# Output projection as seven products of quarter matrices instead of eight

## The chip, the cores and the metric

The kernel runs on one core of one Trainium2 chip. The metric is the device time of one execution in microseconds (us). The engines are named as in the profile: PE is TensorE's matmul, PEld its weight load, DVE is VectorE, ACT is ScalarE, POOL is GpSimd, and SP is SyncE, which here only issues transfers (DMAs).

## What is computed

One layer of a decoder trunk over 1024 positions of width 1024, all in float32. Two token mixers (A and B) give `y_A` and `y_B`, learned gates merge them, and the merged matrix is projected. The change is in that projection and in what feeds it:

```python
m_a, m_b = jnp.split(jax.nn.sigmoid(h @ w_merge[i]), 2, axis=-1)
out = (m_a * y_a + m_b * y_b) @ w_out[i]          # (1024, 1024) @ (1024, 1024)
x = x + rmsnorm(out, g_post[i])
e = p[i] @ w_ple[i]
gate = jax.nn.sigmoid(x @ w_ple_gate[i])
x = x + rmsnorm(gate * e, g_ple[i])
```

## The kernel before

**How it is scheduled.** The kernel writes its operations into a list (`Program`, lines 198 to 552), and a planner (`schedule`, from line 301) turns the list into a fixed order for each engine. The planner takes the operation that can start first by its own costs and latencies, places tiles in two arenas in on-chip memory (`arena_r` for float32r operands, `arena_f` for float32) and in the eight banks of PSUM (`arena_p`), and keeps to the quotas of the table `QUOTA`. `BASE` gives each part its rank. All instructions are emitted from line 521, so the profile has one line for nearly everything, and a reader goes by engine, tile and shape. An engine runs its own list in order: an instruction that waits holds up all that stand behind it.

**Precision by three products.** A float32 matrix is split in a high part (a cast to float32r) and a low part (source minus high), by `split_w` for a source in on-chip memory and `split_p` for one in PSUM. The cast may go to ACT or DVE, and `split_w`'s subtraction to POOL or DVE, as the planner likes. `mm3` then issues three matmuls. A block of 128 rows by 512 columns with a depth of 1024 thus takes 24 matmuls of 512 columns.

**The parts of the program.** `p2_block` and `score_block` (parts "x" and "s", the first 110 us) make the keys and the sparse-attention scores: for each of eight row blocks a projection of 208 columns, a chain of small DVE operations on it (names `wi`, `fb`, `cs`), transposes, then the score matmuls, which ACT passes through a Relu and DVE adds up. `v_b`, `q_a`, `gates_a`, `merge_gates`, `pair_b`, `top_k` and `mixer_a` fill the middle. Then, for each half `t` of the rows, `y_A` and `y_B` are made in 8 column blocks, merged and split into `mt`. A small product (`pe`) follows, then the output projection: columns in two halves `q`, for each half eight row blocks `b`, each 24 matmuls into one bank, then

```python
        V.scalar_tensor_tensor(x1[b][:, cq], ps, 0.25, gpb[:, cq], op0=ALU.mult, op1=ALU.mult)
        A.activation(jo, ps, AF.Square, scale=0.25, accum_out=s1[:, b, q:q + 1])
```

With the second half a block's norm is finished, the residual `x` is loaded and added, and the result is transposed and split into `xT`, which the last stage (the gate with `w_ple_gate`, 16 blocks of 24 matmuls) reads. `load_q` loads half of a weight matrix in four transfers of 512 KB and splits it.

Of the kernel before, what the change touches and what calls it, by code (L numbers as in the profile page):

```python
# [12 lines left out]
F32 = mybir.dt.float32  # L13
F32R = mybir.dt.float32r
# [536 lines left out]
class _Eng:  # L551
# [11 lines left out]
    "hT": (64, 0, 1, 64, 1), "w2": (14, 0, 0, 14, 1), "wn": (36, 1, 1, 16, 1), "vbt": (8, 1, 0, 4), "W": (16, 0, 0, 4, 1),  # L563
    "Wm": (16, 0, 0, 12), "ki": (8, 0, 0, 8, 1), "hlt": (8, 1, 0, 4, 1), "qs": (6, 1, 0, 4, 1), "kt": (4, 1, 0, 4, 1),
    "B": (48, 1, 0, 32), "pt": (12, 1, 0, 4), "kva": (12, 0, 1, 12), "qsa": (8, 1, 0, 6), "att": (64, 0, 1),
# [9 lines left out]
}  # L575

BASE = {"x": -1, "s": 0.3, "vb": 0.3, "qa": 0.3, "ga": 2.7, "mg": 5.3, "pair": 2, "top": 2.7, "A": 4.7, "end": 6}
STEP = 100000
N_IDLE = 8

# [2 lines left out]
def hybrid_block_kernel(ctx: ExitStack, tc: tile.TileContext, x, p, w_in, b_forget, w_branch_a,  # L583
# [606 lines left out]
    def mixer_a():  # L1190
# [6 lines left out]
        for i in range(NB):  # L1197
# [36 lines left out]
            for g in range(4):  # L1234
                split_w(u4[:, g], at[0, g, 0, t][:, cs_], at[0, g, 1, t][:, cs_])

    pg.at("vb", None)
    v_b()
    pg.at("qa", None)
# [12 lines left out]
    mixer_a()  # L1252


    mt = [[[pg.tile([P, 4, 512], F32R, f"m{t}", f"m{t}{e}{g}") for g in range(2)] for e in range(2)] for t in range(2)]
    for t in range(2):
        pg.at("end", 7 + t)
        c = slice(t * 512, t * 512 + 512)
        for g in range(4):
            for e in range(2):  # L1260
                at[1, g, e, t] = pg.tile([P, 512], F32R, "att", f"at1{g}{e}{t}")
                G.dma_start(at[1, g, e, t], att_d[e][g][t])
        for j in range(8):
            wb = [load_wT(w[0, :, j * P:(j + 1) * P], 4, f"wbr{n}_{j}{t}", "Wb") for n, w in
                  enumerate((w_branch_a, w_branch_b))]
            ths = []
            for mi in range(2):
                th = pg.tile([P, 512], F32, "th", f"thl{mi}_{j}_{t}")
                SY.dma_start(th, th_d[mi][j][:, c])
                ths.append(th)  # L1270
            for mi in (1, 0):
                ps = pg.psum([P, 512], "d", f"y{mi}_{j}_{t}")
                for k in range(4):
                    mm3(ps, *wb[mi][k], at[mi, k, 0, t], at[mi, k, 1, t],
                        k == 0, k == 3, [ths[mi]] if k == 0 else ())
                V.scalar_tensor_tensor(ths[mi], ths[mi], 1.0, ps, op0=ALU.add, op1=ALU.mult)
            V.tensor_add(ths[0], ths[0], ths[1])
            split_w(ths[0], mt[t][0][j // 4][:, j % 4], mt[t][1][j // 4][:, j % 4])


    QW = 512
# [1 line left out]
    def load_q(src, q, name):  # L1283
        ws = []
        sv = src.rearrange("(k p) c -> p k c", p=P)
        for k in range(0, KC, 2):
            w = pg.tile([P, 2, 2, QW], F32R, "wo", f"{name}{k}")
            st = pg.tile([P, 2, QW], F32, "st", f"{name}s{k}")
            SY.dma_start(st, sv[:, k:k + 2, q * QW:(q + 1) * QW], hold=[w])
            split_w(st, w[:, 0], w[:, 1])  # L1290
            ws += [(w[:, 0, 0], w[:, 1, 0]), (w[:, 0, 1], w[:, 1, 1])]
        return ws
# [42 lines left out]
    pg.at("end", 10)
    wq, begun = {}, []
    for q, b in order:
        if q not in wq:
            wq[q] = load_q(w_out[0], q, f"wo{q}")
        cq = slice(q * QW, (q + 1) * QW)  # L1340
        ps = pg.psum([P, 512], "d", f"out{q}_{b}")
        begun.append(len(pg.ops))
        t, bs = b // 4, slice((b % 4) * P, (b % 4 + 1) * P)
        for k in range(KC):
            mm3(ps, mt[t][0][k // 4][:, k % 4, bs], mt[t][1][k // 4][:, k % 4, bs], *wq[q][k],
                k == 0, k == KC - 1, [x1[b]] if k == 0 else ())
        V.scalar_tensor_tensor(x1[b][:, cq], ps, 0.25, gpb[:, cq], op0=ALU.mult, op1=ALU.mult)
        A.activation(jo, ps, AF.Square, scale=0.25, accum_out=s1[:, b, q:q + 1])
        if q == 1:
            xb = []  # L1350
            for g in range(2):
                xb.append(pg.tile([P, 512], F32, "xr", f"xr{b}{g}"))
                SY.dma_start(xb[g], x[0, b * P:(b + 1) * P, g * 512:(g + 1) * 512])
            V.tensor_add(s1[:, b, 4:5], s1[:, b, 0:1], s1[:, b, 1:2])
            A.activation(s1[:, b, 5:6], s1[:, b, 4:5], AF.Sqrt, scale=1.0 / D, bias=eps_t)
            V.reciprocal(s1[:, b, 4:5], s1[:, b, 5:6])
            for g in range(2):
                xg = x1[b][:, g * 512:(g + 1) * 512]
                V.scalar_tensor_tensor(xg, xg, s1[:, b, 4:5], xb[g], op0=ALU.mult, op1=ALU.add)
                pt = pg.psum([P, 4, P], "t", f"xt{b}_{g}")  # L1360
                with pg.group():
                    for c in range(4):
                        T.transpose(pt[:, c], x1[b][:, (4 * g + c) * P:(4 * g + c + 1) * P], ident)
                split_p(pt, xT[t][0][g][:, :, bs], xT[t][1][g][:, :, bs])


    C3 = 0.375 ** 6
# [16 lines left out]
    for n, (q, b) in enumerate(order):  # L1384
        if q not in wq:
            wq[q] = load_q(w_ple_gate[0], q, f"wg{q}")
        cq = slice(q * QW, (q + 1) * QW)
        t, bs = b // 4, slice((b % 4) * P, (b % 4 + 1) * P)
        ps = pg.psum([P, 512], "d", f"pg{q}_{b}")
        begun.append(len(pg.ops))  # L1390
        for k in range(KC):
            mm3(ps, xT[t][0][k // 4][:, k % 4, bs], xT[t][1][k // 4][:, k % 4, bs], *wq[q][k],
                k == 0, k == KC - 1)
        gv = gvs[q, b] = pg.tile([P, QW], F32, "gv", f"gv{q}_{b}")
        SY.dma_start(gv, ge_d[b][:, cq])
        pg.ops[-1].deps.add(begun[13 + n])
        th = pg.tile([P, QW], F32, "gt", f"gt{q}_{b}")
        A.activation(th, ps, AF.Tanh, scale=0.5)
        last = q == 1 and b == NB - 1
        if last:  # L1400
            A.activation(warm, th[:, 0:1], AF.Sqrt, scale=0.0, bias=eps_t)
        V.scalar_tensor_tensor(gv, th, 1.0, gv, op0=ALU.add, op1=ALU.mult)
        if q == 1:
            V.tensor_tensor_reduce(out=jo, in0=gv, in1=gv, scale=0.25, scalar=s2[:, b, 0:1], op0=ALU.mult, op1=ALU.add,
                                   accum_out=s2[:, b, q:q + 1])
        else:
            A.activation(jo, gv, AF.Square, scale=0.5, accum_out=s2[:, b, q:q + 1])
# [59 lines left out]
```

## Time and profile before

| | |
|---|---|
| median of three runs (lowest, highest) | 1111.01 us (1108.54, 1111.92) |
| the profiled execution's own time | 1111.12 us |
| its span in the trace | 1109.4 us |
| PE busy, DVE busy, ACT busy, POOL busy | 97%, 72%, 54%, 12% of the span |
| mean granted clock of TensorE | 0.986 of full speed |

The span runs from the first to the last recorded instruction; 1.7 us of the time lie outside it. Busy shares are means over stages with different limits, so a stage is read by its own window.

### The profile page before, as it was taken

To read this page: it belongs to the slowest core of one execution; us is meant where nothing else is said; L and a number is where in the kernel's file an instruction comes from. 1 tells how busy PE (TensorE), PEld (TensorE's weight loads), DVE (VectorE), ACT (ScalarE), POOL (GpSimd) and SP (SyncE) were. 2 spreads that over 40 slices of the span, in tenths; PEclk is the share of its full clock that TensorE was granted. 3 is DMA by queue.
4 is the path that set the end of the run, shared out by engine and by line. 5 is a ranking of instruction groups with operands and counts; after the bars stand their busy time and mean duration, and the time that the engine had idled before them with its cause. 6 is when DMAs were issued, how large, how long until landed. Compare 5 with 4: busy or idle time off the path is not lost. (4 is left out here: it accounts for less than half of the span.)

```text
span 1109.4 us, 16308 instructions
## 1 busy us (share of the span) xinstructions
PE 1073.3 (97%) x5290; PEld 882.7 (80%) x5290; DVE 802.1 (72%) x2086; ACT 603.8 (54%) x1396; POOL 133.2 (12%) x244
## 2 busy tenths in 40 slices
PE   8899999999999999999999999999999999999995
PEld 6777887887878878788878888888888888887884
DVE  6999667757969878799999957655388732366277
ACT  6565578888889889775278855432112131233212
POOL 1413000010111211211411200000100000000011
PEclk8999999999999999999999999999999999998998
DMA  7212033370361622635243422333786273026032
GB/s 264 70 37 67 11 138 119 134 180 10 102 156 39 159 70 82 150 97 178 95 124 97 122 64 79 106 113 106 227 247 200 77 242 109 29 72 202 31 111 99
DMA packets 117594, 128.00 MB, mean 115 GB/s; under 512 B 11642, under 2 KB 78330, under 8 KB 117508
## 3 DMA queue, kind: packets, MB, share of 16 engines
q1 hardware_dynamic: 105940, 108.60, 30.7%
q0 software_dynamic: 11568, 18.35, 7.1%
q8 instruction: 42, 0.69, 0.3%
q14 instruction: 44, 0.36, 0.1%
HBM read 89.60 MB, written 33.13 MB: 111 GB/s over the span
## 5 line engine op out<-in xcount | busy, mean ns | idle before, releaser
L521 PE MATMUL arena_p<-arena_r 128*128 128x512 f32 (+5 forms) x4384 | 1016.0, 385 | 17.1 <-DVE arena_r L521 6.5
L521 PEld LDWEIGHTS arena_p<-arena_r 128*128 128x128 f32 x4384 | 783.8, 190 | 175.6 <-DVE arena_r L521 11.3
L521 ACT ACTIVATE arena_f<-arena_p 128x512 f32<-128x512 f32 (+5 forms) x188 | 97.9, 533 | 205.9 <-PE arena_p L521 123.7
L521 DVE TENSOR_TENSOR arena_r<-arena_p,arena_r 128x512 fp32r<-128x512 f32 (+3 forms) x232 | 141.7, 622 | 48.4 <-ACT arena_r L521 44.7
L521 ACT CAST arena_r<-arena_p 128x512 fp32r<-128x512 f32 (+4 forms) x217 | 107.3, 516 | 117.7 <-PE arena_p L521 114.1
L521 ACT ACTIVATE arena_f<-arena_f,cnd 128x1024 bf16<-128x1024 f32 (+4 forms) x160 | 149.7, 936 | 31.9 <-DVE cnd L521 28.1
L521 ACT ACTIVATE arena_f<-arena_f,stats 128x512 f32<-128x512 f32 (+3 forms) x192 | 116.9, 611 | 21.2 <-DVE stats L521 15.8
L521 DVE TENSOR_TENSOR arena_r<-arena_f,arena_r 128x512 fp32r<-128x512 f32 (+4 forms) x200 | 120.0, 612 | 4.3 <-ACT arena_r L521 1.0
L521 PE MATMUL arena_p<-ident,arena_f 128*128 128x128 f32 x720 | 110.7, 276 | 1.8 <-DVE arena_r L521 0.6
L521 POOL TENSOR_TENSOR arena_r<-arena_f,arena_r 128x512 fp32r<-128x512 f32 (+2 forms) x51 | 65.4, 1289 | 366.2 <-ACT arena_r L521 111.4
L521 PEld LDWEIGHTS arena_p<-ident,arena_f 128*128 128x128 f32 x720 | 87.4, 142 | 24.0 <-DVE arena_f L521 2.3
L521 ACT CAST arena_r<-arena_f 128x512 fp32r<-128x512 f32 (+3 forms) x104 | 55.1, 561 | 69.2 <-DVE arena_f L521 45.8
L521 DVE CAST arena_r<-arena_f 128x512 fp32r<-128x512 f32 (+3 forms) x147 | 55.1, 384 | 41.5 <-DMA arena_f<-in_w_out_dram 15.2
L521 DVE CUSTOM_DVE_ANT_0 arena_f<-arena_p,arena_f 128x512 f32<-128x512 f32 (+2 forms) x112 | 64.1, 577 | 2.6 <-PE arena_p L521 1.5
L521 DVE SCALAR_TENSOR_TENSOR arena_f<-arena_f,wi 128x384 f32<-128x384 f32 (+3 forms) x70 | 48.3, 696 | 13.4 <-ACT arena_f L521 12.6
L521 POOL TENSOR_SCALAR_AFFINE_SELECT arena_f<-arena_f 128x128 f32<-128x128 f32 x70 | 22.5, 323 | 260.5 <-DVE stats L521 112.8
L521 DVE SCALAR_TENSOR_TENSOR arena_f<-arena_f,arena_p 128x512 f32<-128x512 f32 x48 | 32.8, 683 | 28.9 <-PE arena_p L521 22.1
L521 DVE CAST arena_r<-arena_p 128x512 fp32r<-128x512 f32 (+4 forms) x67 | 40.8, 612 | 17.7 <-PE arena_p L521 17.4
L521 ACT COPY arena_f<-arena_p 64x256 f32<-64x256 f32 (+5 forms) x85 | 37.8, 445 | 21.7 <-PE arena_p L521 17.9
L521 DVE SCALAR_TENSOR_TENSOR arena_f<-arena_f 128x512 f32<-128x512 f32 (+7 forms) x47 | 29.0, 623 | 26.5 <-ACT arena_f L521 25.6
L521 DVE TENSOR_TENSOR arena_f<-arena_f 128x512 f32<-128x512 f32 (+3 forms) x101 | 45.0, 446 | 1.3 <-DMA arena_f<-rd_d 0.5
L521 DVE CUSTOM_DVE_ANT_0 arena_f<-arena_p,arena_f,stats 128x384 f32<-128x384 f32 (+2 forms) x64 | 39.3, 615 | 6.9 <-PE arena_p L521 3.6
(103 smaller groups left out, 486.1 us busy)
## 6 DMA issues: line engine op xcount, KB each, us to landing
arena_f<-in_w_in_dram SPq DMA_DIRECT2D x56, 256.0 KB
arena_f<-in_w_merge_dram SPq DMA_DIRECT2D x32, 256.0 KB
th_d<-arena_f SPq DMA_DIRECT2D x32, 256.0 KB
arena_f<-th_d SPq DMA_DIRECT2D x32, 256.0 KB
arena_f<-in_x_dram SPq DMA_DIRECT2D x18, 256.0 KB
vb_d<-arena_r SPq DMA_DIRECT2D x8, 512.0 KB
qsa_d<-arena_r SPq DMA_DIRECT2D x16, 256.0 KB
arena_f<-negc_d SPq DMA_DIRECT2D x8, 512.0 KB
```

The source lines that it names most:

```text
L521: getattr(eng[x], m)(*[real(q) for q in a], **{n: real(q) for n, q in k.items()})
```

## The change

The projection is cut into quarters: the merged matrix A (1024 rows by 1024) into A11, A12, A21, A22 and `w_out` into B11 to B22, each 512 by 512. A product of two quarters takes 4 row blocks of 12 matmuls of 512 columns. Eight such products with four sums of results become seven products of sums of quarters (Winograd's form), with sums before and after:

- T1 to T4 are sums of weight quarters. `weight_sums` makes them early in the program: for each of four row groups `k` two transfers of 512 KB from `w_out`, four subtractions of 128 by 512 on GpSimd, and one transfer of 1 MB to a buffer `tw_d` in DRAM.
- S1 to S4 are sums of quarters of A, made after the merge for the second half of the rows by `either` (GpSimd or DVE). Seven left operands of four tiles are split instead of four.
- `quad` loads one weight quarter or sum in two transfers of 512 KB and splits it; `product` makes one row block. The results are added with `add_to` (DVE, reads PSUM and on-chip memory) into `x1`.
- The squares for the norm now read `x1`, and the weight `g_post` (`gpb`, scaled once) is multiplied in with the norm in `first_residual`, so the residual is added by a separate operation.

```diff
+    pg.at("tw", None)
+    tw_d = [pg.dram(dr, [P, 4, 4, 512], "tw_d0")]
+    def weight_sums(w, dst):
+        for k in range(4):
+            b4 = pg.tile([P, 4, 512], F32, "tw", f"tw{k}")
+            for g in range(2):
+                SY.dma_start(b4[:, 2 * g:2 * g + 2].rearrange("p a b -> p (a b)"), w[(4 * g + k) * P:(4 * g + k + 1) * P, :])
+            G.tensor_sub(b4[:, 0], b4[:, 1], b4[:, 0])
+            G.tensor_sub(b4[:, 1], b4[:, 3], b4[:, 1])
+            G.tensor_sub(b4[:, 3], b4[:, 3], b4[:, 0])
+            G.tensor_sub(b4[:, 2], b4[:, 2], b4[:, 3])
+            SY.dma_start(dst[:, k], b4)
...
-            V.tensor_add(ths[0], ths[0], ths[1])
-            split_w(ths[0], mt[t][0][j // 4][:, j % 4], mt[t][1][j // 4][:, j % 4])
+            m = mq[t][j]
+            V.tensor_add(m, ths[0], ths[1])
+            if t == 0:
+                left["A11" if j < 4 else "A12"].append(halves(m, "mA", f"mA{j}"))
+            elif j < 4:
+                either("tensor_sub", s3[j], mq[0][j], m)
+            else:
+                q = j - 4
+                either("tensor_add", mq[1][q], mq[1][q], m)
+                either("tensor_sub", mq[0][q], m, s3[q])
+                either("tensor_sub", mq[0][j], mq[0][j], mq[0][q])
...
+    def product(lw, i, ws, name, hold=()):
+        ps = pg.psum([P, 512], "d", f"{name}_{i}")
+        for k in range(4):
+            h_, l_ = lw[k]
+            bs = slice(i * P, (i + 1) * P)
+            mm3(ps, h_[:, bs], l_[:, bs], *ws[k], k == 0, k == 3, hold if k == 0 else ())
+        return ps
...
+    def add_to(out_, ps, part):
+        V.scalar_tensor_tensor(out_, ps, 1.0, part, op0=ALU.mult, op1=ALU.add)
...
+    ws = wquad("B11")
+    for i in range(4):
+        A.copy(part[i], product(left["A11"], i, ws, "P1", [x1[4 + i]]))
+    ws = wquad("B21")
+    for i in range(4):
+        add_to(x1[i][:, q0], product(left["A12"], i, ws, "P2", [x1[i]]), part[i])
+        square(i, 0)
+    ws = wquad("T2")
+    for i in range(4):
+        add_to(part[i], product(left["S2"], i, ws, "P6"), part[i])
+    ws, ws2 = wquad("T1"), wquad("B22")
+    for i in range(4):
+        add_to(late[i], product(left["S1"], i, ws, "P5"), part[i])
+        add_to(x1[i][:, q1], product(left["S4"], i, ws2, "P3"), late[i])
+        square(i, 1)
+        first_residual(i)
+    ws = wquad("T3")
+    for i in range(4):
+        ps = product(left["S3"], i, ws, "P7")
+        add_to(late[i], ps, late[i])
+        add_to(part[i], ps, part[i])
+        square(4 + i, 1)
+    ws = wquad("T4")
+    for i in range(4):
+        add_to(part[i], product(left["A22"], i, ws, "P4"), part[i])
+        square(4 + i, 0)
+        first_residual(4 + i)
```

The tables change with it: the buffer for the residual `x` (`"xr"`) grows from 2 to 4 KB, `"we"` from 12 to 16 KB, `"m0"` and `"m1"` give way to `"mA"`, `"mS"` and `"mq"`, and `"tw"` has 8 KB, one tile of four sums.

**What moves.** The planner makes a new order for every engine, since it is greedy and the early part differs. On GpSimd's list, in the first 110 us, these are the rows from the end of the setup to the selects on the first scores (`AFFINE_SELECT`); a row that writes `arena_r` is the low part of a split, one that writes `arena_f` from `arena_f` is a sum of weight quarters:

```order
 L521 TENSOR_TENSOR arena_r<-arena_f,arena_r 128x4x128
-L521 TENSOR_TENSOR arena_r<-arena_f,arena_r 128x512 x9
-L521 TENSOR_TENSOR arena_r<-arena_f,arena_r 128x4x64 x3
+L521 TENSOR_TENSOR arena_r<-arena_f,arena_r 128x512
+L521 TENSOR_TENSOR arena_f<-arena_f 128x512
+L521 TENSOR_TENSOR arena_r<-arena_f,arena_r 128x512 x2
+L521 TENSOR_TENSOR arena_f<-arena_f 128x512 x3
+L521 TENSOR_TENSOR arena_r<-arena_f,arena_r 128x512 x3
+L521 TENSOR_TENSOR arena_f<-arena_f 128x512 x4
+L521 TENSOR_TENSOR arena_r<-arena_f,arena_r 128x4x64
 L521 AFFINE_SELECT arena_f<-arena_f 128x128
+L521 TENSOR_TENSOR arena_f<-arena_f 128x512 x4
```

The 16 sums stand in four batches of four among the early splits (the last batch follows behind the next select), and some of the splits' low parts have gone to DVE.

On SP's list, at the end of the output projection, these are the rows before of the residual loads (`in_x`) and of the first weights of the gate (`in_w_ple_gate`):

```order
L521 DMA arena_f<-in_x_dram 128x512 x8
L521 DMA arena_f<-ge_d_156 128x512
L521 DMA arena_f<-in_x_dram 128x512 x2
L521 DMA arena_f<-ge_d_157 128x512
L521 DMA arena_f<-in_x_dram 128x512 x2
L521 DMA arena_f<-ge_d_158 128x512
L521 DMA arena_f<-in_x_dram 128x512
L521 DMA arena_f<-in_w_ple_gate_dram 128x2x512 x2
```

And these after:

```order
L521 DMA arena_f<-in_x_dram 128x512 x4
L521 DMA arena_f<-tw_d_146 128x2x512
L521 DMA arena_f<-in_x_dram 128x512 x3
L521 DMA arena_f<-in_w_ple_gate_dram 128x2x512
L521 DMA arena_f<-in_x_dram 128x512
L521 DMA arena_f<-in_w_ple_gate_dram 128x2x512 x3
```

Before, 14 of the 16 residual loads stand ahead of the gate's first weights (one of them further up); after, nine do (two of them further up), and the four transfers of the gate's first half follow almost at once.

## Rows read from the trace of the kernel before

**Rows 1.** The page: busy time of TensorE's matmuls, share, instructions

```profile
PE 1073.3 (97%) x5290; PEld 882.7 (80%) x5290; DVE 802.1 (72%) x2086; ACT 603.8 (54%) x1396; POOL 133.2 (12%) x244
```

**Rows 2.** Waits of PE, whole span: us in total, times, longest

```profile
PE arena_p L521 <- DVE arena_r L521: 10.0, 13, 2.7
PE arena_p L521 <- DVE arena_f L521: 7.3, 8, 2.4
```

**Rows 3.** Windows: length, busy (instructions) by engine, PEclk, DMA share, GB/s

```profile
50.00:100.00 50.00, 49.34 (x251) 38.50 (x250) 46.23 (x172) 30.36 (x77) 10.25 (x11) 1.00 0.21 59
850.00:1015.00 165.00, 161.13 (x728) 130.97 (x727) 83.25 (x135) 40.17 (x88) 2.60 (x2) 0.98 0.35 117
```

**Rows 4.** Timeline of PE: start, length, instructions [idle before <-releaser]

```profile
899.17 61.93 PE L521 MATMUL arena_p<-arena_r 128*128 128x512 f32 x272 [0.23 <-DVE arena_r L521]
...
1004.56 0.80 PE L521 MATMUL arena_p<-arena_r 128*128 128x512 f32 x1 [2.34 <-DVE arena_r L521]
1005.75 2.50 PE L521 MATMUL arena_p<-arena_r 128*128 128x512 f32 x5 [0.40 <-DVE arena_r L521]
...
1015.07 81.21 PE L521 MATMUL arena_p<-arena_r 128*128 128x512 f32 x357
```

**Rows 5.** Windows of 3 us where the granted clock is low

```profile
109.00:112.00 3.00, 2.60 (x11) 2.37 (x12) 2.89 (x6) 1.74 (x4) 1.88 (x1) 0.65 0.00 0
112.00:115.00 3.00, 3.00 (x16) 2.67 (x15) 1.65 (x4) 0.98 (x2) 0.00 (x0) 0.78 0.02 5
...
1006.00:1009.00 3.00, 3.00 (x10) 2.41 (x11) 1.49 (x2) 0.00 (x0) 0.00 (x0) 0.50 0.72 208
1009.00:1012.00 3.00, 3.00 (x11) 2.35 (x11) 2.20 (x3) 0.59 (x1) 0.00 (x0) 0.66 0.88 322
```

**Rows 6.** Timeline of POOL, 30 to 110 us

```profile
31.29 1.29 POOL L521 TENSOR_TENSOR arena_r<-arena_f,arena_r 128x512 fp32r<-128x512 f32 x1 [1.52 <-ACT arena_r L521]
33.27 7.33 POOL L521 TENSOR_TENSOR arena_r<-arena_f,arena_r 128x512 fp32r<-128x512 f32 x5 [0.69 <-ACT arena_r L521]
50.25 1.34 POOL L521 TENSOR_TENSOR arena_r<-arena_f,arena_r 128x512 fp32r<-128x512 f32 x1 [9.66 <-DVE arena_r L521]
56.05 1.29 POOL L521 TENSOR_TENSOR arena_r<-arena_f,arena_r 128x512 fp32r<-128x512 f32 x1 [4.46 <-ACT arena_r L521]
...
103.93 3.25 POOL L521 TENSOR_TENSOR arena_r<-arena_f,arena_r 128x512 fp32r<-128x512 f32 x2 [3.08 <-DVE arena_r L521]
```

**Rows 7.** Timeline of DVE, 30 to 110 us

```profile
31.48 2.48 DVE L521 TENSOR_TENSOR arena_r<-arena_p,arena_r 128x512 fp32r<-128x512 f32 x4
...
35.56 1.23 DVE L521 TENSOR_SCALAR wi<-arena_f 128x8 f32<-128x8 f32 x1
...
40.87 0.15 DVE L521 TENSOR_SCALAR wi<-arena_f 128x8 f32<-128x8 f32 x1
...
103.71 0.61 DVE L521 SCALAR_TENSOR_TENSOR arena_f<-arena_f,wi 128x384 f32<-128x384 f32 x1
...
104.38 1.66 DVE L521 SCALAR_TENSOR_TENSOR arena_f<-arena_f,wi 128x384 f32<-128x384 f32 x1
```

**Rows 8.** Timeline of PE, 40 to 110 us

```profile
42.81 0.73 PE L521 MATMUL arena_p<-identr,arena_r 128*128 128x128 f32 x4 [2.69 <-DVE arena_r L521]
...
59.60 0.28 PE L521 MATMUL arena_p<-identr,arena_r 128*128 128x128 f32 x1 [0.16 <-DVE arena_r L521]
...
109.40 0.62 PE L521 MATMUL arena_p<-arena_r 128*128 128x384 f32 x2 [1.89 <-ACT arena_f L521]
```

**Rows 9.** DVE by form, 840 to 1015 us: busy us, mean ns of one

```profile
L521 DVE TENSOR_TENSOR arena_r<-arena_f,arena_r 128x1024 fp32r<-128x1024 f32 x12 | 14.6, 1220 | 0.3
...
L521 DVE SCALAR_TENSOR_TENSOR arena_f<-arena_p,arena_f 128x512 f32<-128x512 f32 x16 | 11.1, 692 | 36.0 <-PE arena_p L521 34.7 <-ACT arena_f L521 0.9
...
L521 DVE TENSOR_TENSOR arena_f<-arena_f 128x512 f32<-128x512 f32 x9 | 6.2, 688 | 0.2
```

**Rows 10.** Transfers, 0 to 64 us in 40 slices: GB/s

```profile
GB/s 0 252 191 320 133 312 379 412 412 231 323 415 415 399 327 45 0 0 0 0 0 10 10 0 0 41 0 0 103 126 343 206 283 87 37 91 82 51 75 48
```

More of the change, by code (lines that the diff above doesn't have):

```diff
@@ L572 @@
     "x1": (32, 0, 1, 32), "gv": (24, 1, 0, 18), "es": (8, 1, 0, 2), "g": (4, 1, 0), "pb": (2, 1, 0, 1), "gt": (4, 1, 0, 2),
[1 row of a table removed]
[1 row of a table added]
     "o": (12, 1, 0, 2), "d": (8, 0, 0, 2, 1), "is": (2, 1, 0, 2, 1), "pe": (8, 1, 0, 2), "rk": (6, 1, 0, 6),
 }
[L577 removed]
+BASE = {"x": -1, "s": 0.3, "vb": 0.3, "qa": 0.3, "ga": 2.7, "mg": 5.3, "tw": 4.0, "pair": 2, "top": 2.7, "A": 4.7, "end": 6}
 STEP = 100000
@@ L1252, in hybrid_block_kernel, with halves @@
     mixer_a()
-    mt = [[[pg.tile([P, 4, 512], F32R, f"m{t}", f"m{t}{e}{g}") for g in range(2)] for e in range(2)] for t in range(2)]
+    def halves(src, grp, name):
+        hl_ = [pg.tile([P, 512], F32R, grp, f"{name}{e}") for e in range(2)]
+        split_w(src, *hl_)
+        return hl_
+    mq = [[pg.tile([P, 512], F32, "mq", f"mq{t}{j}") for j in range(8)] for t in range(2)]
+    s3 = [pg.tile([P, 512], F32, "mq", f"ms{j}") for j in range(4)]
+    left = {n: [] for n in ("A11", "A12", "S1", "S2", "S3", "S4", "A22")}
     for t in range(2):
@@ L1333, in hybrid_block_kernel @@
     jo = pg.tile([P, QW], BF16, "jk", "jo")
-    order = [(q, b) for q in range(2) for b in range(NB)]
[L1335 to L1364, printed above, removed]
@@ new lines, in hybrid_block_kernel, with quad @@
+    V.tensor_scalar_mul(gpb, gpb, 0.25)
+    pg.at("end", 10)
+    for n, src in (("S2", mq[0][:4]), ("S1", mq[1][:4]), ("S4", mq[0][4:]), ("S3", s3), ("A22", mq[1][4:])):
+        for k in range(4):
+            left[n].append(halves(src[k], "mS", f"{n}{k}"))
+    begun = []
+    def quad(w, tw, n):
+        ws = []
+        for k in range(0, 4, 2):
+            if n[0] == "B":
+                g, q = int(n[1]) - 1, int(n[2]) - 1
+                src = w.rearrange("(k p) c -> p k c", p=P)[:, 4 * g + k:4 * g + k + 2, q * 512:q * 512 + 512]
+            else:
+                src = tw[:, k:k + 2, ("T1", "T3", "T4", "T2").index(n)]
+            wt = pg.tile([P, 2, 2, 512], F32R, "wo", f"w{n}{k}")
+            st = pg.tile([P, 2, 512], F32, "st", f"w{n}s{k}")
+            SY.dma_start(st, src, hold=[wt])
+            split_w(st, wt[:, 0], wt[:, 1])
+            ws += [(wt[:, 0, 0], wt[:, 1, 0]), (wt[:, 0, 1], wt[:, 1, 1])]
+        return ws
@@ new lines, in product, with square, first_residual @@
+    def product(lw, i, ws, name, hold=()):
+        ps = pg.psum([P, 512], "d", f"{name}_{i}")
+        begun.append(len(pg.ops))
+        for k in range(4):
+            h_, l_ = lw[k]
+            bs = slice(i * P, (i + 1) * P)
+            mm3(ps, h_[:, bs], l_[:, bs], *ws[k], k == 0, k == 3, hold if k == 0 else ())
+        return ps
+    def square(b, q):
+        A.activation(jo, x1[b][:, q * 512:q * 512 + 512], AF.Square, scale=0.25, accum_out=s1[:, b, q:q + 1])
+    def first_residual(b):
+        t, bs = b // 4, slice((b % 4) * P, (b % 4 + 1) * P)
+        xb = []
+        for g in range(2):
+            xb.append(pg.tile([P, 512], F32, "xr", f"xr{b}{g}"))
+            SY.dma_start(xb[g], x[0, b * P:(b + 1) * P, g * 512:(g + 1) * 512])
+        V.tensor_add(s1[:, b, 4:5], s1[:, b, 0:1], s1[:, b, 1:2])
+        A.activation(s1[:, b, 5:6], s1[:, b, 4:5], AF.Sqrt, scale=1.0 / D, bias=eps_t)
+        V.reciprocal(s1[:, b, 4:5], s1[:, b, 5:6])
+        for g in range(2):
+            xg = x1[b][:, g * 512:(g + 1) * 512]
+            V.scalar_tensor_tensor(xg, xg, s1[:, b, 4:5], gpb[:, g * 512:(g + 1) * 512], op0=ALU.mult, op1=ALU.mult)
+            either("tensor_add", xg, xg, xb[g])
+            pt = pg.psum([P, 4, P], "t", f"xt{b}_{g}")
+            with pg.group():
+                for c in range(4):
+                    T.transpose(pt[:, c], x1[b][:, (4 * g + c) * P:(4 * g + c + 1) * P], ident)
+            split_p(pt, xT[t][0][g][:, :, bs], xT[t][1][g][:, :, bs])
@@ new lines, in add_to, with wquad @@
+    def add_to(out_, ps, part):
+        V.scalar_tensor_tensor(out_, ps, 1.0, part, op0=ALU.mult, op1=ALU.add)
+    def wquad(n):
+        return quad(w_out[0], tw_d[0], n)
+    q0, q1 = slice(0, 512), slice(512, 1024)
+    part, late = [x1[4 + i][:, q0] for i in range(4)], [x1[4 + i][:, q1] for i in range(4)]
+    ws = wquad("B11")
[5 more added lines that the diff above has]
+        square(i, 0)
@@ L1395, in hybrid_block_kernel @@
         SY.dma_start(gv, ge_d[b][:, cq])
-        pg.ops[-1].deps.add(begun[13 + n])
+        pg.ops[-1].deps.add(begun[25 + n])
         th = pg.tile([P, QW], F32, "gt", f"gt{q}_{b}")
```

1 line of the change is left out of this document (added), and 6 rows, old and new, of the table QUOTA.

## The prediction, made before the change was run

> **What bounds the kernel now.** I read the page first: TensorE's matmuls are busy for 1073.3 of 1109.4 us [rows 1]. The list of what TensorE waited for comes next. Its two largest entries, 17.3 us in 21 waits, both name VectorE [rows 2]. So the end is set by the amount of matmul work and by the places where VectorE is late. The windows then show where VectorE has room: hardly any in 50 to 100 us (46.23 of 50 busy), much from 850 to 1015 us, where the change adds its sums (83.25 of 165) [rows 3].
>
> The reader should see two more things. First, where TensorE stands still for 2 us or so, its granted clock may fall behind the wait. The 1.89 us wait at 109.40 [rows 8] is followed by two windows at 0.65 and 0.78, and the 2.34 and 0.40 us at 1004 [rows 4] by 0.50 and 0.66 [rows 5]; 0.50 is the lower level (1.2 of 2.4 GHz) throughout. The 2.69 us at 42.81 had no such price. Second, GpSimd and VectorE get in each other's way. While GpSimd subtracts 128x512 tiles (five from 33.27 to 40.6 us; one alone takes 1.29) [rows 6], VectorE's little operation on `wi` takes 1.23 us, and the same operation 0.15 us at 40.87, just after GpSimd stopped; an addition of scores takes 1.66 instead of 0.61 us when GpSimd runs its pair at 103.93 [rows 6, 7]. The difference, 1.05 to 1.08 us, is a standstill. VectorE's operations that read PSUM are spared: four from 31.48 to 33.96 took 0.62 us each, with GpSimd at work to 32.58 and from 33.27 [rows 6, 7].
>
> **The change, part by part.**
>
> *Matmuls.* Seven products of 48 take the place of eight, and the order shows 48 matmuls of 512 columns fewer, 3680 for 3728, with every other form unchanged. In the unbroken run of the gate 357 took 81.21 us, 0.2275 each; the projection gives the same (272 in 61.93) [rows 4]. That is **-10.9 us**, all on the path, because TensorE is the busy engine there (161.13 of 165) [rows 3].
>
> *The early sums.* The loads and stores are 8 MB in the first 110 us. The queue is nearly empty from 25 to 44 us, but moves some 400 GB/s before that [rows 10]; the first 1 MB comes behind the last `x` and would cost 2.6 us at that rate if it delayed work. I take 0, since the pieces of `w_in` behind it are wanted only by the score products at 48 us. The first store, 1 MB, waits on SP for its batch of sums; behind it stand a `w_in` piece and the key stores, wanted later still. Also 0.
>
> The price is VectorE's. Sixteen subtractions of 1.29 us stall it by at most 16 x 1.08 = 17.3 us. Four low parts fewer go to GpSimd in this stretch and cost VectorE 0.61 each instead of a 1.08 stall: 1.9 back, so 15.4 net, and at the lower end 0, where VectorE would have been idle. How much TensorE pays, batch by batch:
>
> - Batch 1. The run of splits that ended at 40.6 gets four sums and loses one split; one sum fits in a gap. Two more stalls, 2.2 us, and TensorE was already waiting there (2.69 at 42.81 [rows 8]), so all of it counts.
> - Batch 2 falls in the chain of small operations on `p2_block`, 43 to 60 us. It stalls 4.3 us; the splits at 50.25 and 56.05 move away (-2.2) and two of them cost VectorE 0.61 each (+1.2). Of the 3.3 us, TensorE has 1.4 of cover: the new order puts 57 instead of 51 matmuls of 512 columns between the transposes of this stretch. The two single stalls before cost TensorE only 0.16 us (59.60 [rows 8]), so a little slack exists. I take 2.0.
> - Batches 3 and 4 fall among the score additions. The nearest row is the pair at 103.93, which was followed by TensorE's 1.89 us wait for ScalarE, itself held up by VectorE [rows 6, 8]. Four in a row cost at least that, at most 4.3. I take 1.9 each, the lower end, because VectorE was not quite full there, and 1.0 back because the pair itself moves.
>
> Together **+7.0 us**, bounds 0 and 15.4. For the clock behind such waits I add one fall like that at 109: (0.35 + 0.22) x 3 us = **+1.7** [rows 5], bounds 0 and 3.4.
>
> *Sums, splits and squares at the end.* VectorE gets 12 more additions from PSUM (0.692), 27 more of 128x512 (0.688), five more low parts of that size and three of 1024 columns (1.220): 8.3 + 18.6 + 3.4 + 3.7, some 34 us [rows 9]; five casts fewer are left out. From 850 to 1015 it is busy 83.25 [rows 3], so some 117 of the 154 that are left there: hidden on the whole. In the alternation of P5 and P3 one row block gives TensorE 24 x 0.2275 = 5.5 us and its transposes, VectorE two additions, two norms, two residual additions and two splits, some 5.4 us: tight, with gate products behind to fill in. At the lower end this costs 0, at the upper one wait like that at 1004. I take **+1.5**.
>
> *The gate's weights.* Before, 14 residual loads stood ahead of the gate's first weights, TensorE waited 2.34 and 0.40 us for their split and then ran at 0.50 and 0.66: 2.74 + (0.50 + 0.34) x 3 = 5.3 us [rows 4, 5]. In the new order the weights come earlier, and 48 gate matmuls instead of 27 stand ahead of the last block's transposes, so more is there to cover the last norm. I take two thirds, **-3.5**, bounds 0 and -5.3.
>
> Sum, from the profiled execution's own 1111.1 us: 1111.1 - 10.9 + 7.0 + 1.7 + 1.5 - 3.5 = **1106.9 us**. The median of the runs is 0.1 lower, which changes nothing.
>
> **The rivals.** A difference of 0.3%, 3.3 us, is about what a measurement of this kernel can tell from none: faster is below 1107.7, slower above 1114.3.
>
> *GpSimd's sums stop VectorE and TensorE pays all of it.* For it: VectorE is 92% busy at 50 to 100 us [rows 3], and the static order knows nothing of the stall. Against: two single stalls cost 0.16 us. Then 15.4 and two falls of the clock, 3.4: 1111.1 - 10.9 + 15.4 + 3.4 + 1.5 - 3.5 = 1117.0. It decides for slower once stalls and clock together cost over 16.1 us, some 1.0 us per sum. The Trainium skill (SBUF — State Buffer, section "SBUF: two separate sides") says that VectorE and GpSimd share a port pair by an exclusive lock, held for the whole instruction, which stops a VectorE operation with two inputs in on-chip memory. The trace agrees (1.23 for 0.15 us); by that rule alone 16 x 1.29 = 20.6 us of VectorE's time would go.
>
> *The new stage pays for its dependences.* The sums at P5 and P3, or a quarter's weights, come late once, at the price of the wait at 1004, and nothing is won at the gate: 1111.1 - 10.9 + 8.7 + 5.3 = 1114.2; half of that price gives 1111.6: no change. For it: the tight 5.4 against 5.5 us. Against: each quarter's weights can load a product (10.9 us) ahead.
>
> *The sums are hidden.* VectorE's early work is not what TensorE needs: 1111.1 - 10.9 + 1.5 - 3.5 = 1098.2. Against it speak the waits at 42.81 and 109.40.
>
> That the products are not removed is excluded by the count in the order.
>
> **How the numbers follow.** The forecast has 0.46 (0.36 of it below 1107.7, 0.10 above), the hidden sums 0.12, the new stage's price 0.24 (0.20 no change, 0.04 slower), the full stall 0.18 (0.16 slower). So faster 0.48, same 0.32, slower 0.20. The forecast alone spans 1102 to 1110: stalls of 2 to 10 us. The range that leaves out 2 in 10 runs from 1099.5, just above the hidden case, to 1116, just short of the full stall.
>
> **What would show it.** Right: 48 matmuls fewer at 0.2275; VectorE operations of 1.2 us beside GpSimd's sums in 30 to 100 us; TensorE's waits up to 110 us longer by about 7, with perhaps one more low clock; no wait of over 2 us at the start of the gate. Wrong if TensorE reaches 110 us's work no later than before, if waits of over 2 us appear among the seven products, or if the new order of the middle part, which the planner also made anew, gains or loses several microseconds, for which no row gives a price.

## The result, and the profile after

The changed kernel takes **1121.3 us** (median of 4, 1120.8 to 1122.4), the kernel before 1110.4 beside it: a ratio of 1.010 (95% interval 1.0082 to 1.0118). It is slower, and outside the predicted range. The profiled execution's span is 1120.6 us. (Of all executions in this document one, of experiment 8, was slow, 1181.0 us at a granted clock of 0.844, and is left out.) The same views as before, first the page and the waits of TensorE:

```profile
PE 1068.2 (95%) x5242; PEld 872.6 (78%) x5242; DVE 851.4 (76%) x2129; ACT 622.3 (56%) x1421; POOL 185.6 (17%) x277
```

```profile
PE arena_p L521 <- DVE arena_r L521: 18.5, 17, 3.8
PE arena_p L521 <- DVE arena_f L521: 7.9, 9, 2.5
PE arena_p L521 <- ACT arena_f L521: 5.3, 10, 1.6
PE arena_p L521 <- DVE stats L521: 4.2, 5, 1.9
```

The 48 matmuls are gone [rows 1], but TensorE stands still for 52.4 us instead of 36.1 (span less busy), and its waits for VectorE grew from 17.5 us (17.3 in [rows 2], 0.2 for `stats`) to 30.6 in these rows. Its timeline, in the early part and at the end:

```profile
43.51 0.87 PE L521 MATMUL arena_p<-identr,arena_r 128*128 128x128 f32 x4 [3.77 <-DVE arena_r L521]
...
66.24 0.25 PE L521 MATMUL arena_p<-identr,arena_r 128*128 128x128 f32 x1 [3.67 <-DVE arena_r L521]
...
89.92 0.96 PE L521 MATMUL arena_p<-arena_r 128*128 128x512 f32 x3 [1.57 <-ACT arena_f L521]
...
924.51 55.55 PE L521 MATMUL arena_p<-arena_r 128*128 128x512 f32 x243 [1.48 <-ACT arena_f L521]
...
1030.85 76.46 PE L521 MATMUL arena_p<-arena_r 128*128 128x512 f32 x336
```

The waits at 43.51 and 66.24 answer to those of 2.69 and 0.16 us [rows 8]. The one at 89.92, at the end of a batch of sums, is of other matmuls than the 1.89 us at 109.40 [rows 8] (512 columns, not 384). At the end no wait is longer than 1.48 us, and the gate starts without the 2.34 and 0.40 us of before [rows 4]. GpSimd's sums and what VectorE did beside them:

```profile
59.36 5.96 POOL L521 TENSOR_TENSOR arena_f<-arena_f 128x512 f32<-128x512 f32 x4
...
84.39 5.91 POOL L521 TENSOR_TENSOR arena_f<-arena_f 128x512 f32<-128x512 f32 x4
```

```profile
85.63 0.47 DVE L521 TENSOR_SCALAR arena_f<-arena_f,wi 128x512 f32<-128x512 f32 x1
86.03 1.26 DVE L521 TENSOR_TENSOR arena_f<-arena_f 128x8 f32<-128x8 f32 x1
...
87.74 1.43 DVE L521 SCALAR_TENSOR_TENSOR arena_f<-arena_f,wi 128x512 f32<-128x512 f32 x1
89.10 0.68 DVE L521 CAST arena_r<-arena_p 128x512 fp32r<-128x512 f32 x1
```

All four of VectorE's rows lie inside the batch from 84.39 to 90.30. The two with two operands in SBUF are stretched, the tiny one to 1.26 us and the large one to 1.43; the one with a single tile operand and the one that reads PSUM are not. This is the standstill of [rows 6, 7]. The granted clock then falls behind the first two waits (windows of 3 us; columns as in [rows 3]; before, it fell at 109 instead [rows 5]):

```profile
43.00:46.00 3.00, 2.49 (x13) 2.43 (x13) 3.00 (x26) 0.95 (x4) 0.00 (x0) 0.50 0.30 89
46.00:49.00 3.00, 3.00 (x16) 3.00 (x16) 2.23 (x17) 0.00 (x0) 0.00 (x0) 0.50 0.64 174
...
67.00:70.00 3.00, 2.97 (x9) 2.30 (x10) 2.96 (x18) 1.83 (x7) 0.00 (x0) 0.50 0.16 40
```

VectorE's additions at the end came about as forecast in number, 27 and 11 more than in [rows 9] (by form, 840 to 1015 us); those in SBUF took 0.82 us each instead of 0.69, and their stretch still had room (127.24 of 165 us busy from 850 to 1015):

```profile
L521 DVE TENSOR_TENSOR arena_f<-arena_f 128x512 f32<-128x512 f32 x36 | 29.0, 820 | 0.4
...
L521 DVE SCALAR_TENSOR_TENSOR arena_f<-arena_p,arena_f 128x512 f32<-128x512 f32 x27 | 18.3, 685 | 8.4 <-PE arena_p L521 7.3 <-ACT arena_r L521 0.9
```

The place of the loss shows best in two long windows, where the matmuls counted in brackets tell how far the work has come. Before, then after:

```profile
0.00:125.00 125.00, 115.44 (x653) 93.64 (x654) 107.69 (x331) 74.61 (x176) 31.08 (x79) 0.96 0.31 97
125.00:760.00 635.00, 625.47 (x3157) 516.54 (x3156) 498.17 (x1384) 450.73 (x1060) 85.37 (x144) 1.00 0.37 107
```

```profile
0.00:125.00 125.00, 108.32 (x604) 87.23 (x605) 110.39 (x319) 69.54 (x165) 46.20 (x87) 0.95 0.51 166
125.00:760.00 635.00, 617.83 (x3094) 504.60 (x3093) 498.33 (x1383) 450.10 (x1059) 87.23 (x150) 0.99 0.36 102
```

By 125 us the changed kernel is 49 matmuls behind, at the window's mean of 115.44/653 = 0.177 us some 8.7 us: about what was forecast for the sums and the clock. But from 125 to 760 us, where no sum and no product of the change runs, it loses 63 more, at 625.47/3157 = 0.198 us some 12.5 us. (Such a count mixes matmuls of different sizes, so these are estimates.) There only the order of the work is new.

### The profile page after: what moved, and what is told of

Same layout as the page of the kernel before. It is cut to its first block, busy times and chain, and to the rows that moved or that the text cites. A ratio compares the mean times of both kernels' runs of the same rounds, so it can differ in the third digit from the quotient of the medians.

```text
span 1120.6 us, 16392 instructions
## 1 busy us (share of the span) xinstructions
PE 1068.2 (95%) x5242; PEld 872.6 (78%) x5242; DVE 851.4 (76%) x2129; ACT 622.3 (56%) x1421; POOL 185.6 (17%) x277
## 5 line engine op out<-in xcount | busy, mean ns | idle before, releaser
L521 PEld LDWEIGHTS arena_p<-arena_r 128*128 128x128 f32 x4336 | 774.5, 190 | 184.8 <-ACT arena_f L521 16.0
L521 ACT ACTIVATE arena_f<-arena_p 128x512 f32<-128x512 f32 (+4 forms) x172 | 88.5, 529 | 145.6 <-PE arena_p L521 120.3
L521 DVE TENSOR_TENSOR arena_r<-arena_p,arena_r 128x512 fp32r<-128x512 f32 (+2 forms) x232 | 141.1, 621 | 37.1 <-ACT arena_r L521 34.2
L521 ACT CAST arena_r<-arena_p 128x512 fp32r<-128x512 f32 (+3 forms) x217 | 106.8, 514 | 107.5 <-PE arena_p L521 102.2
L521 POOL TENSOR_TENSOR arena_r<-arena_f,arena_r 128x512 fp32r<-128x512 f32 (+3 forms) x63 | 87.2, 1390 | 436.1 <-ACT arena_r L521 224.4
L521 DVE TENSOR_TENSOR arena_r<-arena_f,arena_r 128x512 fp32r<-128x512 f32 (+4 forms) x206 | 132.2, 652 | 7.7 <-ACT arena_r L521 3.9
L521 ACT CAST arena_r<-arena_f 128x512 fp32r<-128x512 f32 (+3 forms) x125 | 73.6, 612 | 87.1 <-DVE arena_f L521 32.1
L521 DVE CAST arena_r<-arena_f 128x512 fp32r<-128x512 f32 (+3 forms) x144 | 54.5, 385 | 46.6 <-PE arena_p L521 17.3
L521 DVE TENSOR_TENSOR arena_f<-arena_f 128x512 f32<-128x512 f32 (+3 forms) x128 | 68.7, 541 | 2.8 <-DMA arena_f<-rd_d 1.7
L521 POOL TENSOR_TENSOR arena_f<-arena_f 128x512 f32<-128x512 f32 (+1 forms) x29 | 38.6, 1331 | 137.2 <-ACT arena_f L521 86.4
L521 DVE CAST arena_r<-arena_p 128x512 fp32r<-128x512 f32 (+3 forms) x67 | 41.7, 623 | 17.6 <-PE arena_p L521 16.6
```

The source lines that it names most:

```text
L521: getattr(eng[x], m)(*[real(q) for q in a], **{n: real(q) for n, q in k.items()})
```

## The experiments

Two theories to begin with. **Theory 1:** the sums hold VectorE up, and this lateness costs again later, since the order is fixed beforehand. **Theory 2:** the sums cost only early; the middle loses because the planner made a new and worse order. A third blames the transfers or the seven products. All comparisons below are with the kernel before on the same chip (1109.9 to 1110.3 us).

**1. The same order without the subtractions.** In `emit`:

```diff
-        for op in self.order:
+        for op in [o for o in self.order if not (o.var[0][1][0][0] == 'tensor_sub' and o.tiles[0].group == 'tw')]:
```

> The changed kernel's own order, instruction for instruction, with the sixteen subtractions of the weight sums left out (their transfers in and out stay; the four products that should use sums use plain quarters in their place). Theory 1 (the sums hold VectorE up, and this lateness against an order fixed beforehand costs again in the middle part): all that is above the prediction goes with them, 1121.3 - 9.5 (0 to 110 us) - 13.5 (middle part) = about 1098 us. Theory 2 (the sums cost only the early 9.5 us; the middle part loses 13.5 us because its order was made anew and is a worse one): 1121.3 - 9.5 = about 1112 us. Theory 3 (it is the sums' transfers, or the products at the end): 1119 to 1121 us.

Measured: 1105.7 us (0.9952, 0.9935 to 0.9968). Columns as before:

```profile
0.00:125.00 125.00, 119.28 (x683) 97.35 (x684) 106.64 (x338) 77.21 (x181) 23.53 (x72) 0.99 0.51 166
125.00:760.00 635.00, 618.32 (x3102) 505.45 (x3102) 495.27 (x1376) 448.45 (x1056) 86.93 (x149) 0.99 0.36 105
```

The 15.6 us won lie all in the first window (683 matmuls for 604, and the clock at 0.99 for 0.95). The middle is as poor as with the sums, 3102 for 3094: its loss doesn't come from them. The transfers, 166 GB/s, stayed and cost nothing that shows here.

**2. The old order with the sums put in.** At planned times, in `emit` of the kernel before, ahead of each operation:

```diff
+            while ev and op.start >= ev[0][0]:
+                n, k = ev.pop(0)[1], nth // 7
...
+                    eng["G"].tensor_sub(b4[:, o], b4[:, x], b4[:, y])
```

> The kernel before in its own order, with the sums' loads, sixteen subtractions and stores put into the queues of SyncE and GpSimd at the planned times that they have in the changed kernel (the first load 14 us later, since its buffer is not free before); the results are not used. Theory 1: 1110.4 + 9.5 + 13.5 = about 1133 us, with the loss in the middle too. Theory 2: 1110.4 + 9.5 = about 1120 us, the middle part as before. Theory 3 (transfers): 1115 to 1120 us with the loss beside transfers, not beside subtractions.

Measured: 1124.1 us (1.0119, 1.0100 to 1.0138), 14.0 more than before.

```profile
0.00:125.00 125.00, 105.03 (x585) 84.77 (x586) 110.87 (x313) 65.49 (x157) 51.51 (x93) 0.93 0.49 164
125.00:760.00 635.00, 625.00 (x3156) 515.57 (x3156) 501.75 (x1385) 455.13 (x1069) 87.08 (x145) 1.00 0.36 105
```

The loss is early again, 68 matmuls, and more than the 9.5 us that both theories gave to the sums. The middle, in the old order, does not notice that it starts late: 3156 for 3157. Theory 1 falls.

**3. No sums at all.** `weight_sums(...)` left out, the order made anew:

```diff
-    weight_sums(w_out[0], tw_d[0])
...
-                src = tw[:, k:k + 2, ("T1", "T3", "T4", "T2").index(n)]
+                src = w.rearrange("(k p) c -> p k c", p=P)[:, 4 * (k // 4) + k:4 * (k // 4) + k + 2, 0:512]
```

> The changed kernel without the weight sums (no load, subtraction or store; the products read plain quarters of the weights in place of the sums), its order made anew by the planner. Theory 1: 1110.4 - 10.9 (matmuls) - 2 (end stage) = 1097 to 1099 us. Theory 2: 1097 to 1099 us plus whatever the new order of the middle part is worth, which may again be up to 14 us either way. Theory 3: 1098 us if it is the transfers, about 1112 us if it is the products at the end.

Measured: 1095.1 us (0.9855, 0.9838 to 0.9872). Without the sums the planner gives TensorE the old order as far as the last stage (its rows in the trace agree up to 884 us), and the middle is the old one:

```profile
125.00:760.00 635.00, 624.75 (x3155) 516.02 (x3154) 498.13 (x1383) 450.23 (x1059) 85.24 (x144) 1.00 0.37 107
```

So the seven products with this order of the last stage are worth 15.1 us.

**4 and 12. The old kernel in other orders.** The work is unchanged; one guess of the planner moves by 2%:

```diff
-MORE_WAITS = 93.0
+MORE_WAITS = 95.0
```

> The kernel before, computation unchanged, with one of the planner's guesses (what an additional wait costs) at 95 ns for 93 ns, so that only the order changes, from about 300 us on. Theory 1: an order made anew is as good as another, 1110.4 within 2 us. Theory 2: orders differ by luck, the time moves by 4 us or more in either direction. Theory 3: as theory 1.

> The kernel before, computation unchanged, with the planner's guess for an additional wait at 91 ns for 93 ns: another order, different from about 60 us on. If orders differ by luck, the time lies somewhere between 1105 and 1125 us and off 1110.2 by over 2 us; if the 6.8 us at 95 ns were an exception, 1108 to 1112 us.

Measured: 1117.0 us at 95 (1.0052, 1.0031 to 1.0072) and 1113.2 at 91 (1.0022, 1.0009 to 1.0035). The same work costs 7 and 3 us more in orders that nothing in the work asked for. At 95 TensorE's order is the old one up to about 350 us, and the middle loses 33 matmuls, 6.5 us:

```profile
125.00:760.00 635.00, 619.25 (x3124) 508.71 (x3123) 505.53 (x1404) 447.35 (x1047) 83.76 (x143) 1.00 0.36 104
```

**5. Copies in place of subtractions**, in the changed kernel's order:

```diff
+                        m, a = ('tensor_copy', a[:2]) if m == 'tensor_sub' and op.tiles[0].group == 'tw' else (m, a)
```

> The changed kernel's own order, with each of the sixteen subtractions of the weight sums replaced on GpSimd by a copy of the same 128x512 tile, with one operand in place of two (the four products get other quarters than sums). Theory 1a (VectorE is held up by GpSimd's two-operand work): most of the 15.6 us go, 1105 to 1109 us, and VectorE's instructions beside the copies are not stretched. Theory 1b (any GpSimd work of this size on the same tiles holds it up): 1118 to 1121 us.

Measured: 1111.4 us (1.0009, 0.9997 to 1.0021): 5.7 more than without them, between the two forecasts. The four copies of the batch that corresponds to 84.39 take 3.20 us for 5.91, and VectorE's same three instructions beside them:

```profile
78.20 0.47 DVE L522 TENSOR_SCALAR arena_f<-arena_f,wi 128x512 f32<-128x512 f32 x1
78.60 0.57 DVE L522 TENSOR_TENSOR arena_f<-arena_f 128x8 f32<-128x8 f32 x1
...
79.63 0.74 DVE L522 SCALAR_TENSOR_TENSOR arena_f<-arena_f,wi 128x512 f32<-128x512 f32 x1
```

The copies hold VectorE's tiny addition up too, for a shorter time: 0.57 us for 1.26, where an operation of this size on its own takes 0.15 [rows 7]. The large one they do not stretch: 0.74 us is what it takes in experiment 1 with GpSimd idle:

```profile
79.30 0.74 DVE L521 SCALAR_TENSOR_TENSOR arena_f<-arena_f,wi 128x512 f32<-128x512 f32 x1
```

So most of the 15.6 us went, as theory 1a said, but a second operand is not needed to hold VectorE up.

**6 and 7. The sums later.** `pg.at("tw", 8)` and `pg.at("tw", 7)` in place of `pg.at("tw", None)`:

> The changed kernel, with the sums not begun before the end's first stage (some 770 to 840 us, where VectorE is busy for about two thirds of the time), the order of everything before that stage as in the kernel before. Theory 1+2 (the sums cost what they take from a VectorE that TensorE waits for, and the middle loses only where its order is made anew): 1095.1 + 0 to 3 = 1095 to 1098 us. Rival (sixteen subtractions cost their 14 to 16 us wherever they stand): 1109 to 1111 us. Rival (their 8 MB beside the end stage's own transfers is what costs): 1100 to 1105 us, with TensorE waiting for DMA.

> The changed kernel, with the sums at some 580 to 640 us, where VectorE is busy for three quarters of the time; the order is made anew from there to the end. Theory 1+2: 1095.1 + 1 to 8 for the sums, and up to 5 either way for the new order of the second half, 1095 to 1106 us. Rival (the sums cost the same wherever they stand): 1109 us or more.

Measured: 1121.0 us at 8 (1.0105, 1.0085 to 1.0126), against all that I expected, and 1100.1 at 7 (0.9908, 0.9894 to 0.9923), in the range. At 8 the loss lies from 800 to 925 us. There VectorE is not two thirds but 78% busy even without sums (97.31 of 125, experiment 3), so subtractions, transfers and order were all suspects; 10 and 14 below separate them.

**8. The changed kernel in another order**, `MORE_WAITS` at 95 as in 4:

> The changed kernel, computation unchanged, with the planner's guess for an additional wait at 95 ns for 93 ns: the order is made anew from about 90 us on, the sums stay where they are. Theory 2 (the middle's loss is the luck of one order): 1121.3 - 13 to + 5, likely lower, about 1115 us. Rival (any order with the early sums in it loses 13 us in the middle, because the planner does not know that they hold VectorE up): 1119 to 1124 us.

Measured: 1119.5 us (1.0081, 1.0064 to 1.0098). The early sums and a poor middle in this order too: 3099 matmuls from 125 to 760 us, 58 fewer than in the old order, where experiments 4 and 12, planned without sums, have 33 and 31 fewer. Alone this does not decide: the two forecasts overlap from 1119 to 1124 us.

**9. The sums in VectorE's idle time.** Their loads get an earliest planned time:

```diff
-                r = 0.0
+                r = getattr(op, "rel", 0.0)
...
+                pg.ops[-1].rel = 645000.0 + 20000.0 * k
```

> The changed kernel, with the sums' loads held back to a planned 645 us and later, so that the subtractions fall where the run without sums shows VectorE busy for 8 to 13 of 20 us (660 to 780 us) and GpSimd nearly idle; the order before that is that of the kernel before. Theory (sums cost what they take from a VectorE that TensorE waits for): 1095.1 + 0 to 3 = 1095 to 1098 us. Rival (the sums cost at least 5 us anywhere, by their transfers or by the places that their buffer takes): 1100 us or more.

Measured: 1108.5 us (0.9985, 0.9976 to 0.9995), over 10 us above the forecast's 1095 to 1098. The windows of this run (first fence) and of experiment 3:

```profile
640.00:780.00 140.00, 137.94 (x679) 112.18 (x678) 83.11 (x191) 58.53 (x134) 27.07 (x24) 1.00 0.46 153
...
950.00:1030.00 80.00, 71.17 (x328) 57.07 (x328) 70.40 (x102) 34.81 (x69) 19.94 (x8) 0.96 0.51 171
```

```profile
640.00:780.00 140.00, 139.93 (x691) 114.55 (x690) 82.23 (x193) 58.05 (x132) 5.62 (x8) 1.00 0.30 93
...
950.00:1030.00 80.00, 77.71 (x370) 63.45 (x370) 61.78 (x99) 35.95 (x74) 16.86 (x8) 1.00 0.40 134
```

Beside the sums the run loses 12 matmuls, 2.4 us at 0.20, as forecast. Most of the rest, 42 matmuls at 0.21 or 8.8 us, goes after 950 us, where no sum runs, but where the order is new.

**10 and 14. Why experiment 6 lost 26 us against experiment 3.** Experiment 6's order without the subtractions, and then without the sums' transfers too (the same filter as in 1, the second time for every operation on a `tw` tile):

> The order of the run with the sums in the end's first stage, instruction for instruction, without the sixteen subtractions (transfers stay; four products use plain quarters). Theory a (there too it is the subtractions: VectorE turned out to be busy for 17 to 18 of 20 us from 800 us on): 1096 to 1103 us. Theory b (the 8 MB beside a stage that has its own 250 to 330 GB/s to move, and the waits that they put into SyncE's queue): 1112 to 1121 us.

> The order of the run with the sums in the end's first stage, without subtractions and without their loads and stores (four products use plain quarters). If the 20 us lost between 825 and 925 us are the transfers': 1096 to 1102 us. If they are the order's, made anew there: 1114 to 1118 us.

Measured: 1117.7 us (1.0069, 1.0054 to 1.0084) and 1116.5 us (1.0058, 1.0039 to 1.0077). Of the 1121.0, subtractions make 3.3 and transfers 1.2 (the last within the runs' spread). The rest, 21 us above the 1095.1 of experiment 3, is the order, which was planned with the sums just ahead of the products that read them. 800 to 925 us without any sums (experiment 14, first fence) and in experiment 3:

```profile
800.00:925.00 125.00, 111.60 (x458) 88.69 (x457) 89.99 (x145) 25.15 (x50) 11.59 (x6) 0.93 0.51 159
```

```profile
800.00:925.00 125.00, 122.72 (x545) 100.44 (x545) 97.31 (x147) 33.38 (x60) 17.95 (x11) 1.00 0.59 190
```

TensorE stands still for 11.1 us more there (122.72 less 111.60), and a granted clock of 0.93 for 1.00 costs some 0.07 x 125 = 9 us: together most of the 21.

**11. The early sums with the order held.** Experiment 3 with the insertion of experiment 2:

> The products of the changed kernel in the order that the planner gives them without the sums (to 880 us that of the kernel before), and the sums' loads, subtractions and stores put into the queues of SyncE and GpSimd at the changed kernel's early places; the four products use plain quarters, the sums stay unused. Theory (the parts add up: products -15.1, early sums in the old order +14.0): about 1109 us, no faster than before, and 12 us faster than the changed kernel, whose order was made anew. Rival (the parts don't add; the early sums' lateness is made up or grows with the products): under 1104 or over 1114 us.

Measured: 1108.1 us (0.9982, 0.9973 to 0.9992), for the 1109 expected: the parts add up, and the theory stands.

**13. The whole change, the order held, the sums in VectorE's idle time.** Here the products read the stored sums again, so this is the complete kernel:

```diff
+        ev = sorted((612000 + 14000 * j + d, n, j) for j in range(8)
+                    for n, d in enumerate((0, 475, 4000, 5000, 6000, 7000, 8500)))
```

> The changed kernel complete, in the order that the planner gives it without the sums, instruction for instruction on TensorE, VectorE and ScalarE; the sums are put into the queues of SyncE and GpSimd at a planned 612 to 720 us, as 32 subtractions of 128x256 in a place of the arena that this order leaves free. If the 10 us that the run with the sums at 680 to 745 us lost after 950 us were its new order of the end: 1095.1 + 2 to 4 = 1097 to 1099 us, faster than every version so far. If the sums' transfers to DRAM and back or their waits in SyncE's queue cost: 1102 us or more.

Measured: **1097.5 us** (0.9892, 0.9878 to 0.9907), the fastest complete kernel of the study, 12.7 us under the kernel before and 23.8 under the changed one. It does all the work of the change, its transfers too; what differs is the order, the sums' place and their cut into 32 halves of 128x256. Beside the sums it loses 12 matmuls against experiment 3, and after 950 us none (371 for 370):

```profile
640.00:780.00 140.00, 138.24 (x679) 112.38 (x679) 85.99 (x191) 56.69 (x130) 31.05 (x40) 1.00 0.49 149
...
950.00:1030.00 80.00, 77.73 (x371) 63.46 (x370) 61.33 (x99) 37.15 (x75) 17.08 (x8) 1.00 0.42 138
```

## Why the prediction was wrong

Four runs make a square: the seven products with the order held or made anew, with the sixteen early subtractions or without.

| median, us | no subtractions | early subtractions | their price |
|---|---|---|---|
| old order held | 1095.1 (experiment 3) | 1108.1 (experiment 11) | +13.0 |
| order made anew | 1105.7 (experiment 1) | 1121.3 (the change) | +15.6 |
| price of the new order | +10.6 | +13.2 | |

(Experiment 1 keeps the sums' transfers, 3 does not have them.) "Held" is the old order up to the last stage; the order of the last stage had to be made anew for the products in all four. From the kernel before: 1110.2 - 15.1 (products) + 13.0 (early sums) + 13.2 (new order) = 1121.3.

*Matmuls, -10.9: right.* 48 fewer, at 76.46/336 = 0.2276 us.

*The end stage, +1.5 and -3.5: right in sum.* With the order held the products gave 15.1 where 10.9 + 3.5 - 1.5 = 12.9 was forecast. No wait of 2 us stands at the gate or among the products. The traces say where the other 2 us come from. TensorE's last matmuls in experiment 3 are

```profile
1075.80 7.19 PE L521 MATMUL arena_p<-arena_r 128*128 128x512 f32 x31
```

They end at 1082.99 us, 13.3 us before those of the kernel before (1015.07 + 81.21 = 1096.28 [rows 4]): the 12.9. From there to the end of the span (1093.6 and 1109.4 us) it takes 10.6 us in experiment 3 and 13.1 before. This end is long in the changed kernel (1120.6 - 1107.31 = 13.3) and in experiment 1 (13.2), which have one order, and short in experiments 11 and 13 (10.7 both), which have that of experiment 3. So some 2.5 us belong to an order of the end and not to the products, and the changed kernel did not get them. Why the end is shorter in one order was not followed up.

*The early sums, +7.0, and the clock, +1.7: the right mechanism, mis-sized.* Measured 13.0 to 15.6 for 8.7, between the forecast and the rival by which TensorE pays all of it (15.4 + 3.4 = 18.8). The first windows of experiment 1 and of the change divide the 15.6: TensorE stands still for 119.28 - 108.32 = 11.0 us more, where 7.0 was forecast, and a clock of 0.95 for 0.99 costs some 0.04 x 125 = 5 us, where 1.7 was. The prediction gave VectorE slack beside batches 2 to 4; there was hardly any. Batch 2 was to cost 2.0 behind 1.4 of cover: TensorE waited 3.67 us at 66.24, and the clock fell behind it. The rival's point of decision, 1.0 us per sum, was nearly reached: 13.0/16 = 0.8 in the held order, 15.6/16 = 0.98 in the new one. (One row was read too simply: the 1.23 for 0.15 us that the prediction sets beside a rule for two inputs belongs to an operation with one tensor operand; the row with two is the addition, 1.66 for 0.61 [rows 7].) The 8.7 us of 125 us seemed to confirm the forecast only because the new order, without the sums, is 30 matmuls ahead of the old one there (683 for 653), some 5 us.

*The transfers, 0: as far as the runs show, right.* The first window of experiment 1 carries them and is the best of all, though in an order of its own.

*The order: the step that failed.* The prediction took the new order of the middle part at nothing: "or if the new order of the middle part, which the planner also made anew, gains or loses several microseconds, for which no row gives a price". The new order, of the whole kernel, cost 10.6 to 13.2 us, nearly as much as the sums: it wins some 5 us before 125 us and loses 10 to 12 from 125 to 760 us; 2.6 more lie behind the last matmul. Without it the result would have been 1108.1 us, inside the range; that this lies so near 1106.9 is luck, since the sums cost 4.3 us more than forecast and the end gave 2.2 more. What is worse in this order is located, not explained. From 125 to 760 us TensorE's waits in the kernel before are

```profile
PE arena_p L521 <- DVE arena_f L521: 5.7, 5, 2.4
PE arena_p L521 <- DVE arena_r L521: 3.2, 6, 1.7
PE arena_p L521 <- DVE stats L521: 0.2, 1, 0.2
```

some 9 us, and in experiment 1 some 16, 4.2 of them for `stats`, just as in the change:

```profile
PE arena_p L521 <- DVE arena_r L521: 6.8, 9, 2.2
PE arena_p L521 <- DVE stats L521: 4.2, 5, 1.9
PE arena_p L521 <- DVE arena_f L521: 4.1, 3, 2.5
PE arena_p L521 <- ACT arena_f L521: 0.7, 2, 0.5
```

Behind one of these waits the granted clock falls once more than before, in the change at 345 us (in experiment 1 at 327, to 0.77 and 0.67); in the kernel before it falls once from 125 to 760 us, behind a wait at 262 us:

```profile
345.91 20.60 PE L521 MATMUL arena_p<-arena_r 128*128 128x512 f32 x84 [2.13 <-DVE arena_r L521]
```

```profile
345.00:348.00 3.00, 2.09 (x6) 1.67 (x7) 2.82 (x9) 1.42 (x3) 0.00 (x0) 0.78 0.00 0
348.00:351.00 3.00, 3.00 (x10) 2.41 (x9) 2.23 (x5) 2.90 (x6) 0.00 (x0) 0.66 0.00 0
```

That is (0.22 + 0.34) x 3 = 1.7 us; with the 625.47 - 617.83 = 7.6 us by which TensorE stands still longer, some 9 of the middle's 12.5 us are accounted for.

Experiments 4 and 12 speak for chance, though they don't prove it: orders made anew for a changed guess lost 7 and 3 us. But the two orders that were planned with the early sums in them, the change's and experiment 8's, lose about twice as many matmuls in the middle (63 and 58) as those two (33 and 31), so it may also be that early sums lead this planner to a worse order; no run tells the two apart. Which of the planner's choices does it stays open.

The expectations had their own miss: I thought that late sums would be cheap and the order nearly free. The first holds (2.4 us between 640 and 780 us, 3.3 in the last stage); the second did not, and hid the first in experiments 6 and 9.

## What to carry to other kernels

Where a planner writes the order, a change is two changes: the work, and a new order of everything behind the first row that moved. Give the new order a price and a range of its own, from the old kernel planned again with a guess moved by a few per cent (here +3 and +7 us, still less than the 10.6 to 13.2 of the change's own order), and measure the work with the order held, by leaving instructions out or putting them in at emission. Elementwise work on GpSimd is not free beside a full VectorE: put it where VectorE's own share is low, here 13.0 us early against 2.4 between 640 and 780 us.

## What the runs showed of the hardware

- GpSimd's copies hold VectorE up too: sixteen of them cost 5.7 us, sixteen subtractions 15.6, in the same order. The Trainium skill (SBUF — State Buffer, section "SBUF: two separate sides") names any GpSimd operation that reads SBUF as a holder of the shared ports. The trace agrees for the 128x8 addition, which takes 1.26 us beside a subtraction and 0.57 beside a copy; the 128x512 addition was stretched beside a subtraction alone (1.43 us, and 0.74 beside a copy as without one).
- 8 MB of transfers more among the first 110 us (166 for 97 GB/s over the first 125 us) show no delay of TensorE: experiment 1 has 683 matmuls there, the kernel before 653. The orders differ, so a small delay could hide in this.
- A kernel that starts the middle part some 12 us late (experiment 2: 68 matmuls) runs it at the same rate, 3156 for 3157 matmuls: early lateness was neither made up nor paid twice.
